# A hybrid decoder layer: the order in which stick-breaking's values are prepared, and the place at which a recurrence column's weights are rounded

## The chip, the cores and the metric

One core of a Trainium2 chip runs the whole layer as one program. The metric is the device time of one execution in microseconds (us). The engines are named as in the profile: PE (matrix products), PEld (the loading of its weights), DVE (vector), ACT (scalar: copies, casts, activations), POOL (GpSimd) and SP, whose queue issues most DMA transfers.

## The reference

A layer for 1024 tokens of width 1024, with 16 learned tokens (`META`) ahead of them, all in float32. Two feed-forward half steps enclose a mixer, whose single projection `W_in` feeds four recurrence heads (HGRN2) and eight attention heads (stick-breaking).

```python
h = h + 0.5 * swiglu(rms_norm(h, ffn1_norm), ffn1_w_in, ffn1_w_out)
u = rms_norm(h, mix_norm) @ w_in
hq, hf, hi, hg, sq, sk, sv = split(u)
o_hg = hgrn2(hq, hf, hi, hg, lb, hgrn_out_norm)   # S = diag(f) S + (1-f) v^T; o = S^T q
o_sb = stick_breaking(sq, sk, sv, sb_q_norm, sb_k_norm)
#   A[t,s] = sigmoid(z_ts) * prod_{s<j<t} (1 - sigmoid(z_tj)),  z = q.k / sqrt(d)
h = h + concat([o_hg, o_sb]) @ w_out
h = h + 0.5 * swiglu(rms_norm(h, ffn2_norm), ffn2_w_in, ffn2_w_out)
```

In the recurrence f goes through a sigmoid, q and g through x * sigmoid(x), and v enters as it is.

## The kernel before

**Precision.** A float32 product is made of three faster ones: each operand is split into a rounded high part and the rest (`wh`, `wl` for weights, `xh`, `xl` for activations), and PE adds xh·wh, xh·wl and xl·wh (lines 258 to 260). A weight tile is loaded by SP as `raw` (128x1024, line 236), rounded by ACT (`wh`, line 241, the cast spoken of below) and subtracted by DVE (`wl`, line 243). All of this is in `split_w`, which `col_tile` calls for one column tile of `W_in`, that is 128 output columns.

**Stages.** The program runs feed-forward 1 (to about 697 us), the first projections of the mixer, the stick-breaking projections for four pairs of heads p = 0 to 3 (to about 862 us; the last of them with the first recurrence columns), then a *braid* in which attention jobs and recurrence columns take turns on PE (to about 1126 us), a tail, `W_out` (from 1169 us) and feed-forward 2 (from 1280 us).

**Recurrence columns.** `hgrn_fill` goes through 16 columns: v, f, q and g of head 0, then of head 1, and so on (v0, f0, q0, g0, v1 ... g3). Tokens are taken in four `PIECES` for v and f (264, 264, 256, 256) and in two `HALVES` of 512 for q and g. Each piece is a product into one PSUM bank (`proj`), which ACT then empties into a staging tile `st`: a copy for v (line 1144), two sigmoids for f (1150, 1151), a sigmoid for q and g (1158), the last followed by DVE's product with the bank (1159). In the braid there is one such bank. When a column begins, `part` calls `col_tile` for the next column (at the first column for the next two), which loads, casts and subtracts its weights; `ahead_w` keeps them. There are 3 buffers for `wh` and `wl`, 2 for `raw`.

**Attention jobs.** PE makes scores z in one of two banks (1649 to 1652). ACT reads them twice (`keep` at 1655, `sig` at 1656), DVE scans `keep` (1659) and POOL multiplies both (1665). PE then *flips* the weights block by block (a transpose into one of two banks, 1504 and 1558), ACT rounds what it finds there (`wu` and `wm`, 1627), DVE subtracts (1628), and PE multiplies with the values (`oacc`, 1579 and 1581). `olow` and `ot` (1620, 1621) read the result out.

**The values.** `sb_v` is a generator for one pair p: it transposes the projected values `vTs` on DVE by groups of tokens (`vt`), casts them on ACT (`vhl`, 1446), subtracts on DVE (1447) and writes them to DRAM through SP (`vD`, 1454). Its groups are 512 tokens, 512 tokens, and last the 16 learned tokens (a tile of 128x32). Beside it `sb_qk` normalizes q and k and splits them (`ohi`, 1425). Each `yield` gives the turn to other work.

**What sets the order.** PE's instructions stay in the order in which the program lists them (a manual schedule). On the other engines a scheduler picks the order; `issue_after(x)` tells it that what follows comes on its queue behind x.

## Time and profile before

| | |
|---|---|
| median of 3 runs | 1964.71 us (1962.61 to 1965.23) |
| profiled execution | 1965.29 us, with a span of 1963.6 us in the trace |
| busy: PE, DVE, ACT, POOL | 1928.3, 1391.6, 851.7, 449.8 us |
| granted TensorE clock | 1.00 |
| casts at line 241 | 25, of 1052 ns each in the median |
| subtractions at line 243 | 25, of 1226 ns each in the median |

The span runs from the first to the last instruction of the trace; the execution's own time is 1.7 us longer. In a row of a timeline stand the start, the duration, the engine, the line, the operation, output <- inputs, the shapes and how often, and in brackets the idle time of the engine ahead of it with the instruction that ended it. In a row on a whole line stand the least, the median and the largest duration in ns.

### The profile page before, as it was taken

The page shows a single profiled execution, that of the slowest core. Times are in us where ns is not written, and L with a number is a line of the kernel's source. Part 1 is how long each engine was busy: PE and PEld are TensorE (multiplying, and loading weights), DVE is VectorE, ACT ScalarE, POOL GpSimd, SP SyncE. Part 2 cuts the span into 40 slices and gives each one's busy share as a digit, 9 for nine tenths or more (in the row PEclk, how much of TensorE's full clock was granted, in tenths as well). Part 3 has the DMA queues.
Part 4 walks back from the last instruction along what each step waited for, and adds up shares of the span by engine and source line. Part 5 has one row for each costly group of instructions (what it writes and reads, how often), then busy time and mean ns, then how long its engine had stood idle before and what let it go on. Part 6 is the DMA issues. An engine that isn't in the chain of part 4 may idle for free.

```text
span 1963.6 us, 30437 instructions
## 1 busy us (share of the span) xinstructions
PE 1928.3 (98%) x10704; PEld 1622.0 (83%) x10704; DVE 1391.6 (71%) x2186; ACT 851.7 (43%) x1711; POOL 449.8 (23%) x626
## 2 busy tenths in 40 slices
PE   7999999999999999999999999999999999999999
PEld 6888888888888888888888978887888888888887
DVE  6977777877678665567777766667567777767774
ACT  6523343334444544356666635433132332344443
POOL 3010100001000003133333332210544545430000
PEclk9999999999999999999999999999999999999999
DMA  6356787757965415865454167655544444469473
GB/s 211 93 160 174 245 278 237 235 208 280 372 226 185 136 47 144 194 175 148 126 143 126 57 249 216 171 204 181 195 117 140 126 137 119 134 236 330 146 232 113
DMA packets 381688, 355.56 MB, mean 181 GB/s; under 512 B 129040, under 2 KB 284560, under 8 KB 381536
## 3 DMA queue, kind: packets, MB, share of 16 engines
q1 hardware_dynamic: 359728, 288.98, 48.2%
q0 software_dynamic: 20768, 64.63, 9.5%
q8 instruction: 85, 1.39, 0.3%
q14 instruction: 67, 0.55, 0.1%
q10 hardware_dynamic: 1040, 0.00, 0.0%
HBM read 237.95 MB, written 115.57 MB: 180 GB/s over the span
## 4 chain that ended last, share of the span: by engine, by line
PE 91%; DVE 4%; DMA 2%; ACT 2%; issue 1%; POOL 0%; SPq 0%; ACTq 0%; DVEq 0%; POOLq 0%
PE o L741 21%; PE qb L459 18%; PE qc L459 12%; PE qa L459 12%; PE proj L258 5%; PE proj L260 5%; PE proj L259 5%; PE flip L1504 2%; PE wo L259 1%; PE wo L260 1%; PE wo L258 1%; PE mq L1010 1%; PE oacc L1579 1%; PE oacc L1581 1%; PE z L1649 1%
## 5 line engine op out<-in xcount | busy, mean ns | idle before, releaser
L459 PE MATMUL qb<-T,wh 128*128 128x512 f32 x1056 | 344.5, 390 | 1.3 <-ACT T L318 0.8
L459 PEld LDWEIGHTS qb<-T,wh 128*128 128x128 f32 x1056 | 198.1, 188 | 46.1 <-issue 2.5
L459 PE MATMUL qa<-B,wh 128*128 128x512 f32 x696 | 226.8, 391 | 0.0
L258 PE MATMUL proj<-xh,wh 128*128 128x512 f32 (+2 forms) x640 | 213.4, 333 | 2.4 <-ACT st L1151 1.3
L741 PE MATMUL o<-t,w 128*128 128x512 f32 x924 | 211.8, 390 | 0.5 <-DVE u L552 0.5
L260 PE MATMUL proj<-xl,wh 128*128 128x512 f32 (+2 forms) x640 | 209.8, 328 | 0.8 <-DVE xl L1973 0.8
L259 PE MATMUL proj<-xh,wl 128*128 128x512 f32 (+2 forms) x640 | 209.7, 328 | 0.0
L741 PE MATMUL o<-parts 128*128 128x512 f32 x924 | 209.6, 389 | 0.0
L459 PE MATMUL qb<-T,wl 128*128 128x512 f32 x528 | 205.4, 389 | 0.0
L741 PEld LDWEIGHTS o<-t,w 128*128 128x128 f32 x924 | 172.8, 188 | 37.3 <-issue 0.8
L741 PEld LDWEIGHTS o<-parts 128*128 128x128 f32 x924 | 173.4, 188 | 36.0
L371 DVE TENSOR_TENSOR wl<-s,wh 128x512 fp32r<-128x512 f32 x160 | 165.8, 1036 | 50.8 <-ACT wh L369 49.8
L369 ACT CAST wh<-s 128x512 fp32r<-128x512 f32 x160 | 99.7, 624 | 188.5 <-PE qb L459 142.3
L459 PEld LDWEIGHTS qa<-B,wh 128*128 128x128 f32 x696 | 130.6, 188 | 27.3 <-DVE B L845 0.3
L369 ACT CAST wh<-raw 128x512 fp32r<-128x512 f32 x120 | 74.6, 622 | 147.3 <-PE qc L459 99.0
L459 PE MATMUL qa<-B,wl 128*128 128x512 f32 x348 | 135.4, 389 | 0.0
L258 PEld LDWEIGHTS proj<-xh,wh 128*128 128x128 f32 x640 | 120.6, 188 | 14.5 <-ACT st L1151 2.0
L260 PEld LDWEIGHTS proj<-xl,wh 128*128 128x128 f32 x640 | 120.5, 188 | 12.1 <-DVE xl L1973 1.2
L259 PEld LDWEIGHTS proj<-xh,wl 128*128 128x128 f32 x640 | 120.5, 188 | 9.9
L459 PE MATMUL qc<-T,wh 128*128 128x512 f32 x352 | 117.0, 394 | 0.0
L459 PE MATMUL qc<-B,wh 128*128 128x512 f32 x352 | 115.1, 390 | 2.0 <-DVE u L552 1.2
L459 PEld LDWEIGHTS qb<-T,wl 128*128 128x128 f32 x528 | 99.1, 188 | 20.4
(398 smaller groups left out, 3853.9 us busy)
## 6 DMA issues: line engine op xcount, KB each, us to landing
raw<-in_ffn_w_in_dram SPq DMA_DIRECT2D x176, 256.0 KB, 3.9
raw<-in_ffn_w_out_dram SPq DMA_DIRECT2D x112, 256.0 KB, 4.4
w2in<-both SPq DMA_DIRECT2D x28, 512.0 KB, 3.4
raw<-in_w_in_dram SPq DMA_DIRECT2D x25, 512.0 KB, 5.1
ks<-kD SPq DMA_DIRECT2D x32, 260.0 KB, 4.7
wout<-both SPq DMA_DIRECT2D x16, 512.0 KB, 3.8
wh<-w2in SPq DMA_DIRECT2D x27, 256.0 KB, 3.5
wl<-w2in SPq DMA_DIRECT2D x27, 256.0 KB, 3.6
```

The lines of the kernel that those rows point to most:

```text
L258: nc.tensor.matmul(ps, wh[:, s], xs, start=k == 0, stop=False)
L259: nc.tensor.matmul(ps, wl[:, s], xs, start=False, stop=False)
L260: nc.tensor.matmul(ps, wh[:, s], xl[:, k, c0 : c0 + n], start=False, stop=k == nk - 1)
L369: nc.scalar.copy(hi, src)
L371: self.block_lo = nc.vector.tensor_sub(lo, src, hi.bitcast(F32))
L459: nc.tensor.matmul(ps, a[:, k, :], b[:, k, :], start=start and k == 0 and i == 0, stop=k == 3 and i == 2, skip_group_check=True,)
L741: nc.tensor.matmul(banks[bank][m], y[:, m * P : (m + 1) * P], z, start=start and at == 0 and e == 0, stop=q == nq - 1 and e == 2, skip_gro ...
L1010: nc.tensor.matmul(ps[at : at + 32, at_g, :], self.xm[:, 4 * h + k, :], got[i, h][:, k, :], start=h == 0 and kk == 0, stop=h == 1 and kk = ...
L1504: self.nc.tensor.transpose(ps[:m, j, :], src[:, s0 : s0 + m], self.ident)
L1579: nc.tensor.matmul(o[:, c], vj, w[0], start=j == 0, stop=False, skip_group_check=True)
L1581: nc.tensor.matmul(o[:64, c], vj[:, :64], w[1], start=False, stop=end, skip_group_check=True)
L1649: nc.tensor.matmul(z, q, ks[0][:, s0 : s0 + n], start=True, stop=False)
```

## The change

There are two edits. In `hgrn_fill` a column still has its weights loaded when its predecessor begins, always one column ahead now, but the cast and the subtraction are held back (`hold=True` makes `split_w` return a function). They are issued behind the instruction with which ACT empties the predecessor's second piece (v and f) or first half (q and g), which `self.emptied` names. In `sb_v` the learned tokens' group comes first instead of last, and gives up its two turns.

```diff
-    def split_w(self, view, parts=None):
+    def split_w(self, view, parts=None, hold=False):
...
-        hi = self.wp.tile([P, n], F32R, tag="wh", name="wh", bufs=self.w_bufs)
-        if self.split_on_vector:
-            nc.vector.tensor_copy(hi, raw)
-        else:
-            self.rounded = nc.scalar.copy(hi, raw)
-        lo = self.wp.tile([P, n], F32R, tag="wl", name="wl", bufs=self.w_bufs)
-        nc.vector.tensor_sub(lo, raw, hi.bitcast(F32))
-        return hi, lo
+
+        def split(after=None):
+            hi = self.wp.tile([P, n], F32R, tag="wh", name="wh", bufs=self.w_bufs)
+            with self.tc.issue_after(after) if after else ExitStack():
+                if self.split_on_vector:
+                    nc.vector.tensor_copy(hi, raw)
+                else:
+                    self.rounded = nc.scalar.copy(hi, raw)
+            lo = self.wp.tile([P, n], F32R, tag="wl", name="wl", bufs=self.w_bufs)
+            nc.vector.tensor_sub(lo, raw, hi.bitcast(F32))
+            return hi, lo
+
+        return split if hold else split()
...
             if kind == "v":
-                nc.scalar.copy(t, ps)
+                self.emptied = nc.scalar.copy(t, ps).ins
...
-                nc.scalar.activation(k, ps, AF.Sigmoid, scale=-1.0)
+                self.emptied = nc.scalar.activation(k, ps, AF.Sigmoid, scale=-1.0).ins
...
-                nc.scalar.activation(t, ps, AF.Sigmoid)
+                self.emptied = nc.scalar.activation(t, ps, AF.Sigmoid).ins
                 nc.vector.tensor_mul(t, t, ps)
...
-                for c in cols[i + 1 : i + (3 if i == 0 else 2)]:
+                for c in cols[i + 1 : i + 2]:
                     if c not in self.ahead_w:
-                        self.ahead_w[c] = self.col_tile(self.a["w_in"][0], c)
+                        self.ahead_w[c] = self.col_tile(self.a["w_in"][0], c, True)
...
             if half == 1:
                 with self.tc.issue_after(kept["round"]) if i == 0 else ExitStack():
                     use(*plan[i], kept["ps"], c0, n)
+                following = cols[i + 1] if i + 1 < len(plan) else None
+                if ci == (plan[i][0] in "vf") and callable(self.ahead_w.get(following)):
+                    self.ahead_w[following] = self.ahead_w[following](self.emptied)
...
-        for c0, nb, m in ((META, 16, 32), (META + 512, 16, 32), (0, 1, META)):
+        for c0, nb, m in ((0, 1, META), (META, 16, 32), (META + 512, 16, 32)):
...
-            yield 0, 800
+            if c0:
+                yield 0, 800
...
-            yield 0, 1500
+            if c0:
+                yield 0, 1500
```

PE's instructions stand in the same order before and after. On ACT, the place where f0's first pieces are emptied reads before (`ohi` and `vhl` belong to the last stick-breaking pair, `wh` is q0's weights, `st` from the bank are f0's pieces):

```order
L1446 CAST vhl<-vt 128x32
L1425 ACTIVATE ohi<-kT,kg 128x528
L241 CAST wh<-raw 128x1024
L1150 ACT_TABLE_LOAD
L1150 ACTIVATE st<-proj 128x264
L1151 ACTIVATE st<-proj 128x264
L1150 ACTIVATE st<-proj 128x264
L1151 ACTIVATE st<-proj 128x264
L1150 ACTIVATE st<-proj 128x256
```

and after (lines of the changed kernel, where 1150 and 1151 are 1155 and 1156):

```order
L1433 ACTIVATE ohi<-kT,kg 128x528
L1155 ACT_TABLE_LOAD
L1155 ACTIVATE st<-proj 128x264
L1156 ACTIVATE st<-proj 128x264
L1155 ACTIVATE st<-proj 128x264
L1156 ACTIVATE st<-proj 128x264
L244 CAST wh<-raw 128x1024
L1155 ACTIVATE st<-proj 128x256
```

The cast moved from ahead of the table load to behind f0's second piece, and the learned tokens' cast is gone from here.

On DVE, behind q0's first half (`st<-st,proj` is the column's product, the `keep` rows are the scans, `wu` and `wm` the subtractions for flips), before:

```order
L1628 TENSOR_TENSOR wu<-flip,wu 128x2x128
L1159 TENSOR_TENSOR st<-st,proj 128x512
L1659 SCALAR_TENSOR_TENSOR keep<-keep,idle 128x265
L1628 TENSOR_TENSOR wm_7907<-flip,wm_7906 16x256
L1659 SCALAR_TENSOR_TENSOR keep<-keep,idle 128x263
```

and after:

```order
L1638 TENSOR_TENSOR wu<-flip,wu 128x2x128
L1164 TENSOR_TENSOR st<-st,proj 128x512
L246 TENSOR_TENSOR wl<-raw,wh 128x1024
L1669 SCALAR_TENSOR_TENSOR keep<-keep,idle 128x265
L1638 TENSOR_TENSOR wm_7916<-flip,wm_7915 16x256
L1669 SCALAR_TENSOR_TENSOR keep<-keep,idle 128x263
```

The subtraction of g0's weights, which stood ahead of f0's last piece before, now stands between q0's product and the scans. The other columns of the braid follow the same pattern, on ACT behind the half or the piece and on DVE behind the column's own product.

More of the change, by code (lines that the diff above doesn't have):

```diff
@@ L236, in split_w, with col_tile @@
         self.last_load = nc.sync.dma_start(to, view)
-        hi = self.wp.tile([P, n], F32R, tag="wh", name="wh", bufs=self.w_bufs)
-        if self.split_on_vector:
-            nc.vector.tensor_copy(hi, raw)
-        else:
-            self.rounded = nc.scalar.copy(hi, raw)
-        lo = self.wp.tile([P, n], F32R, tag="wl", name="wl", bufs=self.w_bufs)
-        nc.vector.tensor_sub(lo, raw, hi.bitcast(F32))
-        return hi, lo
-    def col_tile(self, w, col):
+        def split(after=None):
[9 more added lines that the diff above has]
+        return split if hold else split()
+    def col_tile(self, w, col, hold=False):
         return self.split_w(
-            w[:, col : col + P].rearrange("(k p) f -> p k f", p=P), self.parted.get(col)
+            w[:, col : col + P].rearrange("(k p) f -> p k f", p=P), self.parted.get(col), hold
         )
```

## The prediction

> **What bounds the kernel now.** The first rows of the page say which engine is full.

> ```profile
> span 1963.6 us, 30437 instructions
> PE 1928.3 (98%) x10704; PEld 1622.0 (83%) x10704; DVE 1391.6 (71%) x2186; ACT 851.7 (43%) x1711; POOL 449.8 (23%) x626
> ```

> PE is busy for 1928.3 of 1963.6 us. The change touches the middle of the program only, so I next read the busy time of each engine by stage (columns: stretch, length, PE, PEld, DVE, ACT, POOL, granted clock, DMA share, GB/s).

> ```profile
> 732.00:862.00 130.00, 128.36 (x779) 114.46 (x779) 72.04 (x111) 58.18 (x111) 34.12 (x53) 1.00 0.66 166
> 862.00:1126.00 264.00, 256.96 (x1817) 228.16 (x1817) 192.81 (x310) 174.28 (x446) 94.77 (x137) 1.00 0.45 126
> 1126.00:1169.00 43.00, 41.04 (x254) 35.21 (x253) 23.84 (x71) 15.18 (x32) 18.54 (x46) 1.00 0.66 235
> ```

> These are the stick-breaking projections, the braid of attention jobs with recurrence columns, and its tail. PE is not busy for 1.64 + 7.04 + 1.96 = 10.6 us in them. ACT is free for a third of the braid (174.28 busy of 264), so ACT work as such costs nothing there; what counts is where it stands when PE next needs a result of ACT or DVE. PE's own waits from 862 to 1169 name these needs (us in total, times, longest):

> ```profile
> PE flip L1504 <- DVE wu L1628: 3.0, 7, 0.7
> PE flip L1504 <- DVE wm L1628: 1.5, 3, 0.6
> ...
> PE z L1649 <- ACT sig L1656: 1.2, 4, 0.5
> ```

> A flip (a transpose of the weights) waits until ACT and then DVE have emptied the flip before it; a z product waits until ACT has read the z two before it. Both chains run through bursts of small ACT and DVE instructions, and the change puts its work into such bursts.

> **The change part by part.** PE's order is unchanged, so its busy time stays, and only its waits can move. Moved are 14 of the 25 roundings of weights (those of the columns q0 to g3) with the subtraction behind each. The two lines over the whole trace, as least, median and most ns of one:

> ```profile
> L241 ACT CAST wh<-raw x25: 1037/1052/1088, 729.6 to 1107.7; 128x1024 fp32r<-128x1024 f32 x25
> L243 DVE TENSOR_TENSOR wl<-raw,wh x25: 1178/1226/2139, 731.0 to 1108.7; 128x1024 fp32r<-128x1024 f32 x25
> ```

> So each move carries 1.05 us of ACT and 1.23 of DVE from one place to another. A place costs PE nothing where the engine would idle; it costs up to 1.05 where ACT is in a chain PE waits for, and up to about 1.5 where the subtraction then stands ahead of DVE's part of the chain too.

> *What leaves.* First, f0's opening piece. The rows in order of time:

> ```profile
> 853.54 1.04 ACT L241 CAST wh<-raw 128x1024 fp32r<-128x1024 f32 x1
> 854.60 1.28 ACT L1150 ACT_TABLE_LOAD   x1
> ...
> 856.18 0.38 ACT L1151 ACTIVATE st<-proj 128x264 f32<-128x264 f32 x1
> ...
> 856.62 0.39 PE L258 MATMUL proj<-xh,wh 128*128 128x256 f32 x1 [1.32 <-ACT st L1151]
> 858.08 0.39 ACT L1151 ACTIVATE st<-proj 128x264 f32<-128x264 f32 x1 [1.23 <-DMA hg_v<-st]
> ```

> PE waits 1.32 for the sigmoid at 856.18, which stands behind the table load, which stands behind q0's cast. That cast now comes behind f0's second piece (the sigmoid at 858.08), so the load can begin at 853.54 rather than 854.60. PE's last matmul before the wait is not moved, so the wait falls to about 0.3: −1.0. The load begins 0.02 us after the cast ends and the sigmoid follows 0.01 behind the load (854.60 + 1.28 = 855.88 against a start of 855.89 on the page's timeline of ACT), so nothing else stands between them.

> [...]

> Next, two old places where the subtraction held DVE ahead of a flip, g1's and g3's:

> ```profile
> 931.17 1.81 POOL L1665 TENSOR_TENSOR sig<-sig,keep 128x912 f32<-128x912 f32 x1 [2.94 <-DVE keep L1659]
> 931.92 2.14 DVE L243 TENSOR_TENSOR wl<-raw,wh 128x1024 fp32r<-128x1024 f32 x1 [0.92 <-ACT wh L241]
> 936.95 0.30 PE L1504 MATMUL flip<-ident,sig 128*128 128x128 f32 x1 [0.67 <-DVE wu L1628]
> 1108.74 1.23 DVE L243 TENSOR_TENSOR wl<-raw,wh 128x1024 fp32r<-128x1024 f32 x1 [0.50 <-ACT wh L241]
> 1111.26 0.41 PE L1504 MATMUL flip<-ident,sig 128*128 128x128 f32 x2 [0.59 <-DVE wm L1628]
> ```

> Without 2.14 and 1.23 us ahead of them, DVE reaches both flips' inputs earlier than PE needs them: −0.67 and −0.59, −1.3 together. What is late next is PE itself. Two more subtractions (q1's, g2's) stand a few us ahead of smaller such waits; I take −0.5 for both, out of the 3.0 that all seven hold. The other old places lie in idle time of ACT or DVE and give nothing.

> Last, the values' generator. The learned tokens' cast (128x32) now comes between the copies of the values' projection, and a copy of kT that PE waits for gets ahead of a long split:

> ```profile
> 780.70 0.19 PEld L258 LDWEIGHTS proj<-xh,wh 128*128 128x128 f32 x1 [0.34 <-ACT kT L1387]
> ```

> That is −0.4 with the slow first matmul behind it. Its four stores move ahead on SP's queue, past the last store of v0's column, which lets that store leave earlier; the work there has cover, and I take 0. The gains are −1.0 − 1.3 − 0.5 − 0.4 = −3.2.

> *What arrives.* Behind the first half of a q or g column and the second piece of a v or f column, ACT now does the cast at once. Behind it are queued, on ACT, the reads of z and the emptyings of flips, and on DVE, behind the subtraction, the products that release the next flip. q0's first half is the clearest place:

> ```profile
> 874.25 0.39 ACT L1655 ACTIVATE keep<-z 128x264 f32<-128x264 f32 x1
> ...
> 874.97 0.42 PE L1649 MATMUL z<-ks,qs 128*128 128x328 f32 x1 [0.48 <-ACT sig L1656]
> ```

> The row of ACT shows no wait before it: the engine goes from the column's half to z without a gap. PE already waits 0.48 for the sigmoid that follows. The cast's 1.05 go straight into the wait: +1.05. Two more bursts are of this kind, behind g0's and q1's first halves, where the z after next starts as the sigmoid ends:

> ```profile
> 897.13 0.55 ACT L1656 ACTIVATE sig<-z 128x456 f32<-128x456 f32 x1
> 897.73 0.43 PE L1649 MATMUL z<-ks,qs 128*128 128x348 f32 x1
> ...
> 964.78 0.54 ACT L1656 ACTIVATE sig<-z 128x456 f32<-128x456 f32 x1
> 965.38 0.43 PE L1649 MATMUL z<-ks,qs 128*128 128x348 f32 x1
> ```

> The sigmoids end at 897.68 and 965.32, 0.05 before the products: +1.0 each.

> Behind g1's, g2's and q3's halves it is DVE's product that PE needs next:

> ```profile
> 984.94 0.68 DVE L1628 TENSOR_TENSOR wu<-flip,wu 128x512 fp32r<-128x512 f32 x1
> 985.68 0.39 PE L1558 MATMUL flip<-ident,sig 128*16 128x128 f32 x2
> ...
> 1073.10 0.42 DVE L1628 TENSOR_TENSOR wu<-flip,wu 128x256 fp32r<-128x256 f32 x1
> 1073.66 0.30 PE L1504 MATMUL flip<-ident,sig 128*128 128x128 f32 x1 [0.61 <-DVE wu L1628]
> ...
> 1140.32 0.41 DVE L1628 TENSOR_TENSOR wm<-flip,wm 16x256 fp32r<-16x256 f32 x1
> 1140.79 0.33 PE L1581 MATMUL oacc<-wm,v 128*64 128x256 f32 x1 [0.26 <-DVE wm L1628]
> ```

> The first of these products ends 0.06 before its flip. With the cast (1.05) and then the subtraction (1.23) ahead of it, less the 0.7 to 0.8 that DVE spends anyway on the column's own product, it comes some 1.5 later: +1.4 for each, +4.2.

> The rest are smaller. I estimate them from the same two prices, 1.05 and 1.4, less the slack that the timelines of PE and DVE leave there. f2's second piece is followed by two flips of which the later needs DVE's product: +0.9. At f1, f3 and q2 the slack takes most: +0.3 each. Behind the pieces of v1, v2 and v3 ACT idles next: 0. That is +1.8; the ends for these seven are 0 and 7 x 1.05 = 7.4. q0's weights are late enough to watch: the sigmoid of 858.08 ends at 858.47, so cast and subtraction end near 860.8, and q0 follows on PE behind f0's last two pieces, some 5.8 us behind the row of 856.62, or 861.4 when 1.0 is saved; I take 0, at 1.0 per us if the load lands late.

> The losses are 1.05 + 2.0 + 4.2 + 1.8 = 9.05, so the net is −3.2 + 9.05 = +5.9 on the profiled execution. Its time was 1965.29 us (span 1963.6 and 1.7 around it), 0.6 over the median of 1964.71. A change in waits carries over to the median: 1964.7 + 5.9 = 1970.6. Some of a new wait is made up, since waits that already follow shrink while DVE catches up; I take 0.6 off for that and forecast 1970.0.

> **The rivals.**

> *The casts hide, and DVE's waits go (faster).* The new place is a fixed one, right after PE has freed the bank and gone on with the next piece. If PE's two z's and the projection matmuls behind them cover 1.05 us, no new wait comes. It decides at the 0.05 us between sigmoid and z at 897.73: the rows speak against it, the free third of ACT for it. Then the gains stand alone, and with the subtractions gone from ahead of the flips up to all of 3.0 + 1.5 go instead of 1.8: −3.2 to −5.9, middle −4.5, or 1960.2.

> *Half of it hides.* Only the places where PE waits already (874.97, 1073.66, 1140.79) lose: 1.05 + 1.4 + 1.4 = 3.85, net +0.6, or 1965.3. For it: these are rows with a wait before, the others are starts that are just in time.

> *Every place loses, and the subtraction stretches.* 14 casts at 1.05 make 14.7. The 2.14 us at 931.92 ran beside POOL's product (931.17 to 932.98), 0.91 over the median; at a few of the new places such a product runs too, and each would add that. −3.2 + 14.7 + 0.9 = +12.4, or 1977. Against it: ACT idles behind the v pieces.

> [...]

> That the change doesn't do what it says is excluded by the order: all 14 casts stand behind their copies.

> **How the numbers follow.** A run can tell about 0.2% from no change, 3.9 us: faster is under 1960.8, slower over 1968.6. Chances: forecast 0.50 (1967 to 1973, of which 0.07 lies under 1968.6), hidden 0.24 (0.15 of it under 1960.8), half 0.18, every place 0.08. Faster 0.15; same 0.07 + 0.09 + 0.18 = 0.34; slower 0.43 + 0.08 = 0.51. The range takes the forecast, the half and the upper part of the hidden case: 1960.8 to 1974.0, which leaves out about 0.15 + 0.07.

> **What would show it.** In the profile after, the wait at f0's second piece is near 0.3 instead of 1.32; z waits of about 1 us stand behind q0's, g0's and q1's first halves; flips wait 1 to 2 us for DVE behind g1's and g2's; PE's total from ACT sig grows from 1.2 to some 4, and the three stages together lose about 6 us while the stages before 732 and after 1169 keep theirs. If z at q0's half waits no longer than 0.5, the hidden case is right and the forecast wrong. If the stages outside change by over 1 us, something that I don't see is at work.

## The result and the profile after

The changed kernel takes 1974.01 us in the median of 6 runs (1969.88 to 1975.10); the kernel before takes 1964.24 (1961.94 to 1966.23). The ratio is 1.0046, with a 95% interval from 1.0033 to 1.0059. The forecast was 1970.0: slower, as foreseen, but by 9.8 us instead of 5.3, above the forecast's own band (1967 to 1973) and at the upper edge of the range. The profiled execution took 1975.1 us, with a span of 1973.4.

The page after, in the two rows that were shown of before:

```profile
span 1973.4 us, 30439 instructions
PE 1933.1 (98%) x10704; PEld 1625.5 (82%) x10704; DVE 1391.0 (70%) x2186; ACT 851.0 (43%) x1711; POOL 448.8 (23%) x626
```

The span grew by 9.8 us, and 4.8 us of it are *busy* time of PE, although PE has the same instructions in the same order. Waits alone don't make PE busy for longer. I come back to this below.

PE's waits from 862 us on (total, times, longest), after:

```profile
PE flip L1514 <- DVE wu L1638: 5.1, 7, 2.1
PE z L1659 <- ACT sig L1666: 3.4, 6, 1.4
PE flip L1568 <- DVE wu L1638: 1.6, 1, 1.6
...
PE oacc L1591 <- DVE wu L1638: 0.9, 1, 0.9
PE flip L1514 <- DVE wm L1638: 0.9, 2, 0.5
```

Flips waited 3.0 + 1.5 for DVE before and wait 5.1 + 1.6 + 0.9 now; z went from 1.2 to 3.4. The single places on PE's timeline, in the order of the prediction's terms (f0, then q0's start, then the new places behind q0, g0, q1, g1, g2 and q3):

```profile
854.12 0.39 PE L263 MATMUL proj<-xh,wh 128*128 128x256 f32 x1 [0.98 <-ACT st L1156]
860.70 0.50 PE L263 MATMUL proj<-xh,wh 128*128 128x512 f32 x1 [0.41 <-ACT st L1156]
...
874.01 0.42 PE L1659 MATMUL z<-ks,qs 128*128 128x328 f32 x1 [1.42 <-ACT sig L1666]
...
897.56 0.43 PE L1659 MATMUL z<-ks,qs 128*128 128x348 f32 x1 [0.68 <-ACT sig L1666]
...
966.06 0.43 PE L1659 MATMUL z<-ks,qs 128*128 128x348 f32 x1 [0.68 <-ACT sig L1666]
987.84 0.39 PE L1568 MATMUL flip<-ident,sig 128*16 128x128 f32 x2 [1.57 <-DVE wu L1638]
...
1079.88 0.30 PE L1514 MATMUL flip<-ident,sig 128*128 128x128 f32 x1 [2.08 <-DVE wu L1638]
...
1148.59 0.33 PE L1591 MATMUL oacc<-wu,v 128*64 128x256 f32 x1 [0.94 <-DVE wu L1638]
```

The six large new waits stand where the prediction put them. f0's wait is 0.98 where it expected about 0.3, and a few smaller waits, such as 0.69 at 951.79 (0.23 before) and 0.21 at 1018.28, are not in it. The rest of the loss is in the clock. These rows are 3.4 us long each, in pairs: ahead of and behind three moments of the changed kernel (columns: stretch, length, busy time of PE, PEld, DVE, ACT, POOL, granted clock, DMA share, GB/s):

```profile
985.60:989.00 3.40, 1.53 (x11) 0.93 (x9) 3.15 (x5) 3.35 (x9) 0.01 (x1) 1.00 0.57 176
989.00:992.40 3.40, 3.01 (x11) 2.65 (x12) 2.82 (x6) 1.55 (x5) 2.19 (x2) 0.50 0.47 133
1077.80:1081.20 3.40, 1.26 (x8) 0.86 (x8) 3.10 (x6) 2.84 (x9) 0.28 (x1) 1.00 0.35 119
1081.20:1084.60 3.40, 3.00 (x9) 2.57 (x10) 1.77 (x4) 1.02 (x3) 3.32 (x4) 0.50 0.60 189
1146.10:1149.50 3.40, 1.91 (x14) 1.26 (x12) 3.01 (x5) 2.25 (x5) 0.00 (x0) 0.99 0.20 77
1149.50:1152.90 3.40, 3.40 (x9) 2.72 (x10) 2.42 (x15) 0.77 (x2) 2.04 (x2) 0.50 0.34 116
```

Behind each of the three places where cast *and* subtraction stand ahead of DVE's product, the clock is halved, to 0.50, for 3.4 us. From 17 us to the last matmul it is nowhere else under 0.99. By these two figures a stretch loses at most 1.7 us. PE's products are longer in it: one of 128x512 at line 264 takes 0.63 us at 991.06, inside, and 0.40 at 993.08, behind it. Set side by side, instruction by instruction, PE's two timelines drift apart by 1.35, 1.37 and 1.46 us in these stretches, 4.2 together. In the kernel before, the same place behind g2's half had a wait of 0.61 and kept its clock:

```profile
1071.60:1075.00 3.40, 2.70 (x19) 1.90 (x17) 2.45 (x5) 3.01 (x9) 0.28 (x1) 1.00 0.20 77
1075.00:1078.40 3.40, 3.02 (x15) 2.59 (x16) 1.66 (x4) 0.99 (x3) 3.32 (x4) 1.00 0.23 77
```

The stretches don't come in every run. The six runs of the changed kernel have a mean clock of 0.997 (1975.10 and 1974.36 us), 0.998 (1973.67 and 1974.65) and 1.000 (1970.90 and 1969.88). A stretch of 3.4 us at half clock takes 0.0009 off the mean (1.7 of some 1970 us), so I take these to be three, two and none; the run of 1975.10 is the profiled one, with its three. The two runs without one lie 6.1 us above the median of before (1970.39 against 1964.24).

### The profile page after: what moved, and what is told of

It is laid out like the page before. It is cut to its first block, busy times and chain, and to the rows that moved or that the text cites. A ratio compares the mean times of both kernels' runs of the same rounds, so it can differ in the third digit from the quotient of the medians.

```text
span 1973.4 us, 30439 instructions
## 1 busy us (share of the span) xinstructions
PE 1933.1 (98%) x10704; PEld 1625.5 (82%) x10704; DVE 1391.0 (70%) x2186; ACT 851.0 (43%) x1711; POOL 448.8 (23%) x626
## 4 chain that ended last, share of the span: by engine, by line
PE 90%; DVE 4%; ACT 2%; DMA 1%; issue 1%; POOL 1%; SPq 0%; DVEq 0%; ACTq 0%; POOLq 0%
PE o L746 21%; PE qb L464 18%; PE qc L464 12%; PE qa L464 12%; PE proj L263 5%; PE proj L265 5%; PE proj L264 5%; PE flip L1514 1%; PE wo L264 1%; PE wo L265 1%; PE wo L263 1%; PE mq L1015 1%; PE oacc L1589 1%; PE oacc L1591 1%; PE z L1659 1%
```

## The experiments

Theory A: the loss comes from the held roundings, as waits at the places named, and as the halved clock behind the longest of them. The rivals were that the moved stores of the values cost the time (B), that the halved clock is a matter of chance and not of waits (C), that POOL and DVE hinder each other (D), and that f0's gain is lost to late weights (E). "Shift" below is the start of an instruction of PE in the experiment less its start in the kernel before; only the differences of shifts along the program are used.

**Each edit alone.** `e1` is the kernel before with the new `sb_v`; `e2` is the changed kernel with the old one.

```diff
 # e1
-        for c0, nb, m in ((META, 16, 32), (META + 512, 16, 32), (0, 1, META)):
+        for c0, nb, m in ((0, 1, META), (META, 16, 32), (META + 512, 16, 32)):
 # e2: the changed kernel, with this line and the two yields turned back
```

> Only the values' edit (learned tokens' group first); the roundings stay free as before. Theory A (the loss comes from the held roundings): within 1.5 us of before; the wait at kT (0.34 at 780.70 before) is gone, the wait at f0's second piece stays about 1.3 less 0.2 for the small cast, no stretch of halved clock. Rival B (the moved stores and the earlier small cast are what costs): 4 us or more slower.

> Only the held roundings; the values' group of the learned tokens stays last. Theory A: 5 to 10 us slower than before, as the changed kernel, with the same waits (z 1.4 behind q0's half; flips 1.6 and 2.1 behind g1's and g2's) and up to three stretches of halved clock. Rival B: at most 3 us slower.

`e1`: 1964.74 us, ratio 1.0003 (0.9994 to 1.0013), so the values' edit makes no difference that can be told. `e2`: 1974.47 us, ratio 1.0054 (1.0037 to 1.0071), the whole loss. Rival B falls. In `e1` the kT wait went as forecast (shift −0.38 by 781 us), and a wait at q0's start took it back and more (+1.24). One expectation missed: the clock was halved for 7 us in the profiled execution of `e1` (1198 to 1205), behind a wait of 1.41 us for a load of `W_out`'s weights; that execution is the slowest of its ten runs, seven of which have a mean clock of 1.000.

`e2` shows f0's term by itself:

```profile
852.81 0.38 PE L263 MATMUL proj<-xh,wh 128*128 128x256 f32 x1 [0.40 <-ACT st L1156]
859.80 0.50 PE L263 MATMUL proj<-xh,wh 128*128 128x512 f32 x1 [0.83 <-ACT st L1156]
...
858.14 1.05 ACT L244 CAST wh<-raw 128x1024 fp32r<-128x1024 f32 x1 [2.69 <-DMA raw<-in_w_in_dram]
```

With the cast gone from ahead of the table load, f0's wait is 0.40 instead of 1.32. The cast, now behind f0's second piece, then waits 2.69 for its load, which is issued one column ahead instead of two, and holds the sigmoids of f0's next pieces behind it on ACT. PE waits 0.83 for the bank.

In the changed kernel the same wait fell to 0.98 only. What ACT does ahead of the table load is the split of kT (`ohi`), and that waits until a store has read the buffer it writes to. The rows of the kernel before, of `e2` and of the changed kernel:

```profile
852.90 0.74 ACT L1425 ACTIVATE ohi<-kT,kg 128x528 fp32r<-128x528 f32 x1 [1.98 <-DMA qD<-ohi]
```

```profile
850.04 0.74 ACT L1433 ACTIVATE ohi<-kT,kg 128x528 fp32r<-128x528 f32 x1 [2.00 <-DMA qD<-ohi]
```

```profile
851.35 0.74 ACT L1433 ACTIVATE ohi<-kT,kg 128x528 fp32r<-128x528 f32 x1 [2.86 <-DMA qD<-ohi]
```

The split starts 2.40, 2.37 and 1.79 us ahead of the moment at which PE runs out of work. With q0's cast gone from behind it, `e2` gains all of 0.9; in the changed kernel the store lands later and takes 0.6 of that back. `e2` and the changed kernel differ in the values' edit alone, so it is this edit that costs the 0.6.

**The three places.** `e3` frees the weights of v2, v3 and g3 in the changed kernel; `e4` holds only these three in the kernel before.

```diff
 # e3
-                        self.ahead_w[c] = self.col_tile(self.a["w_in"][0], c, True)
+                        self.ahead_w[c] = self.col_tile(
+                            self.a["w_in"][0], c, plan[i + 1] not in (("v", 2), ("v", 3), ("g", 3)))
 # e4: the same with "in", the load of two columns ahead at the start, and the old sb_v
```

> The changed kernel, but the weights of v2, v3 and g3 are rounded where the scheduler likes; the other 11 stay held. Theory A (each halved-clock stretch follows from one of these three places, where cast and subtraction stand ahead of DVE's product): the three waits of about 1.5 go (some 4.2 us), the clock is 1.00 in every run and the 1.7 us per stretch go too; in all 4 to 9 us faster than the changed kernel, +1 to +2 against before. Rival C (the halved clock is a state of the chip that comes whatever the waits are): the clock is under 1.00 in some runs still, and only the 4.2 us come back.

> The kernel before, with only the weights of v2, v3 and g3 held behind g1's, g2's and q3's first halves; the other 11 and the values as before. Theory A: +4 in waits at the three places, and 1.7 more for each stretch of halved clock (up to three): 4 to 9 us slower than before, the clock 0.997 to 1.00. Rival C: +4 at most, clock 1.00 as before. If the crowding of all 14 places together is what counts, less than +2.

`e3`: 1969.36 us, ratio 1.0025 (1.0015 to 1.0034), 4.7 us faster than the changed kernel. The clock was 1.00 in all ten runs, and they lie within 2.8 us. But not all of the three waits came back: the freed casts found other places, with waits of 0.84 at 970.82 and 1.25 at 1059.28, so that by the shifts the stage's waits fell by only about 2 us. What `e3` saved is mostly the clock (4.2 in the trace of the changed kernel). That it would come to +1 or +2 against before was wrong; it is +5.0.

`e4`: 1971.66 us, ratio 1.0035 (1.0025 to 1.0046), so three held columns of 14 cost 7.3 us by themselves. With the 5.0 of `e3` that is more than the loss of the changed kernel, so the parts don't simply add up: the three roundings that `e3` frees cost time at other places. All three places of `e4` have their stretch:

```profile
987.30:990.70 3.40, 2.78 (x10) 2.52 (x11) 3.34 (x6) 2.53 (x7) 1.24 (x1) 0.52 0.44 130
1079.20:1083.00 3.80, 3.34 (x12) 2.64 (x11) 3.11 (x6) 1.55 (x5) 3.37 (x2) 0.55 0.51 155
1147.10:1151.10 4.00, 3.73 (x11) 2.94 (x11) 3.09 (x20) 1.09 (x3) 1.94 (x2) 0.60 0.29 98
```

Its runs fall into two groups: three with a mean clock of 0.999, as one stretch makes it (1967.63 to 1969.21, 1968.4 in the mean), and five with 0.997, as three make it (1971.31 to 1973.73, 1972.5 in the mean). Two more stretches go with 4.1 us.

**Cast or subtraction.** `e5` gives the held subtractions of the changed kernel to POOL; the casts stay. `e6` does the same to the kernel before.

```diff
-            nc.vector.tensor_sub(lo, raw, hi.bitcast(F32))
+            (nc.gpsimd if hold else nc.vector).tensor_sub(lo, raw, hi.bitcast(F32))
 # e6: the same for the kernel before, with a flag of its own for these columns
```

> The changed kernel with the 14 held subtractions (wl) on POOL instead of DVE; the casts stay where the change put them. Theory A (cast and subtraction both stand ahead of DVE's product behind g1's, g2's and q3's halves: about 1.05 of cast, 0.5 of subtraction): the flip waits there fall by about 0.5 each, to 1.0 and 1.5, the z waits (1.42, 0.68, 0.68) stay, and with less idle time in a row the halved clock comes less often: 3 to 6 us faster than the changed kernel. Rival D (POOL's subtraction and DVE's work exclude each other): no gain, or slower.

> The kernel before, its order of casts untouched, with the subtractions of the columns' weights on POOL. Theory A (the old places of g1's, q1's, g2's and g3's subtractions cost PE 0.9, 0.3, 0.3 and 0.7 us): these waits go, 1 to 2 us faster than before, at the limit of what can be told. Rival D: the same or slower, since the subtraction takes POOL longer or holds DVE.

`e5`: 1966.08 us, ratio 1.0013 (1.0004 to 1.0022), 8 us faster than the changed kernel and more than expected. POOL's subtraction takes twice as long as DVE's (2390 ns in the median against 1225 in the changed kernel), and nobody waits for it for long:

```profile
L246 POOL TENSOR_TENSOR wl<-raw,wh x14: 2361/2390/2410, 856.2 to 1139.9; 128x1024 fp32r<-128x1024 f32 x14
```

```profile
PE z L1659 <- ACT sig L1666: 3.4, 6, 1.4
PE flip L1514 <- DVE wu L1638: 3.4, 6, 1.2
...
PE flip L1568 <- DVE wu L1638: 0.9, 1, 0.9
```

The z waits (the cast's alone) stay at 3.4, the longest flip wait falls from 2.1 to 1.2, that behind g1 from 1.6 to 0.9, and the clock is 1.00 throughout the profiled execution and in seven of the ten runs (0.999 in three). So the subtraction was 0.6 to 0.9 us of the long waits. From 862 to 1169 us PE's shift grows by 2.6 us here and by 12.0 in the changed kernel: of the 9.4 between them 4.2 are the clock and some 5 are waits, many of them short. Rival D falls. `e6`: 1963.26 us, ratio 0.9997 (0.9988 to 1.0006). Its flips gained some 2.2 us in shift (at 913, 937, 952, 1021 and 1111), but at the braid's start z waited 1.7 in sum and the clock was halved there for 7 us, without any rounding being held; nine of its eleven runs have a mean clock of 0.999 or 0.998. The gain can't be told from no change.

**How long a wait must be.** `e7` holds only g0's, v1's and g1's weights (the z places), `e8` only v3's (one place), `e11` as `e8` with the subtraction done twice.

```diff
 # e7: plan[i + 1] in (("g", 0), ("v", 1), ("g", 1));   e8: plan[i + 1] in (("v", 3),)
 # e11, to e8:
             nc.vector.tensor_sub(lo, raw, hi.bitcast(F32))
+            if hold:
+                nc.vector.tensor_sub(lo, raw, hi.bitcast(F32))
```

> The kernel before with only g0's, v1's and g1's weights held, behind q0's, g0's and q1's first halves, the places where a z product waits for the cast. Theory A: waits of 1.4, 0.7 and 0.7 at z, +2.6 against before less 0.9 for g1's old place; none of them is followed by a stretch of halved clock, so 1 to 3 us slower. Rival C' (any wait over about 0.7 us can set off the halved clock): a stretch behind one of the three places.

> The kernel before with only v3's weights held, behind g2's first half (one place). Theory A: the flip there waits 2.1 instead of 0.6 and one stretch of halved clock of about 3.4 us follows within 2 us of it, which costs 1.7: 1.5 to 3.5 us slower in all. Rival C: the wait without the stretch, +1.5.

> The kernel before with only v3's weights held (as in the run with one place) and the subtraction done twice, so that the flip behind g2's half waits 1.2 us longer, some 3.3 us. Theory A (a long wait sets off the halved clock): a stretch of halved clock of some 3.4 us behind it in the trace, 1.7 us lost, and 4 to 6 us slower than before in all. Rival C (the stretch comes by chance and not by the wait): clock 1.00 at this place and 3 us slower.

`e7`: 1967.30 us, ratio 1.0019 (1.0010 to 1.0028). z waits 1.42, 0.67 and 0.68, and the profiled execution has no stretch; eight of the ten runs have a mean clock of 1.000. It is 3.4 us slower than before, more than the 1 to 3 expected, and flips wait 0.81 twice at 902.63 and 970.97, which wasn't foreseen. `e8`: 1966.46 us, ratio 1.0015 (1.0006 to 1.0024), 2.6 us slower than before, as expected. The wait is the 2.08 of the changed kernel, but in the profiled execution the clock stays at 1.00; there the expectation of a stretch missed. Other runs had one: seven of the ten have a mean clock of 0.999 or 0.998, against 4 of the 33 runs of the kernel before that were taken with them (where in the program it stood, the mean doesn't say). `e11`: 1968.50 us, ratio 1.0022 (1.0013 to 1.0031), with 0.999 or 0.998 in all ten runs. The second subtraction was queued ahead of the next flip's product, so that two waits follow each other, 2.08 and 1.46. Around the place, 3.4 us of `e8`:

```profile
1073.00:1076.40 3.40, 1.27 (x9) 0.86 (x8) 3.09 (x6) 3.35 (x10) 0.00 (x0) 1.00 0.36 124
```

and of `e11`, with what follows:

```profile
1072.00:1075.40 3.40, 1.32 (x10) 0.87 (x8) 3.13 (x5) 3.35 (x9) 0.00 (x0) 0.98 0.20 77
1075.40:1082.00 6.60, 5.14 (x16) 4.03 (x15) 5.31 (x7) 1.50 (x4) 4.59 (x5) 0.50 0.43 128
```

PE is busy for 1.3 of 3.4 us in both. One keeps its clock, the other has it halved for twice 3.4 us. What differs in the two traces is where the wait falls on a beat. In each of the 14 traces every change of the granted clock comes a whole number of steps of 3.4133 us behind its first rise, to within 0.004 us; in the changed kernel, for instance, the rise is at 16.23 (24 transposes from 11.03 on take 5.34 us, 8 from 19.31 on take 1.19), and 989.03, 1081.19 and 1149.46 are 285, 312 and 332 steps behind it. That rise lies anywhere from 13.80 to 17.12 us, so the beat falls differently on the program in each execution. Cut on its beat, `e8` (rise at 15.84) has the wait split over two steps:

```profile
1070.56:1073.97 3.41, 2.45 (x16) 1.83 (x14) 2.22 (x3) 2.13 (x4) 0.62 (x2) 1.00 0.00 0
1073.97:1077.38 3.41, 1.84 (x13) 1.47 (x14) 3.35 (x6) 3.39 (x10) 0.85 (x1) 1.00 0.66 214
```

and `e11` (rise at 17.12) has it whole in one, with the halved clock in the next:

```profile
1071.83:1075.24 3.41, 1.33 (x11) 0.94 (x10) 3.17 (x4) 3.36 (x8) 0.00 (x0) 1.00 0.20 77
1075.25:1078.66 3.41, 1.95 (x8) 1.49 (x8) 3.35 (x7) 1.65 (x5) 2.05 (x2) 0.50 0.63 188
```

So in these two the halved clock goes with a wait, as A has it, and with where the beat falls on it (1.33 us busy in one step, against 2.45 and 1.84 in two), which differs from execution to execution: that is the part of C that holds.

**What became of f0's gain, and a version out of the parts.** `e9` is the changed kernel with f's two outputs of a piece in one staging tile. `e10` is the kernel before with POOL's subtractions, only q0's rounding held (its load two columns ahead as before) and that tile. `e12` is the kernel before with POOL's subtractions for v1 to g3 only.

```diff
 # e9, e10
-            return pool.tile([P, 512], F32, tag="st", name="st", bufs=4)[:, :n]
+            return pool.tile([P, 528], F32, tag="st", name="st", bufs=4)[:, :n]
...
-            t = staged(n)
+            t = staged(2 * n if kind == "f" else n)
...
-                k = staged(n)
+                t, k = t[:, :n], t[:, n:]
 # e12: e6, with the flag True only for i > 2
```

> The changed kernel with f's two outputs of a piece in one staging tile (528 wide, four of them), so that f0's third piece finds a free one. Theory A (f0's earlier sigmoids were given back because ACT waited 4.06 us for a store of hg_k to free a staging tile, and PE 0.41 for the bank at q0): that wait of ACT shrinks to under 1.5 and PE's wait at q0's first matmul goes; f0 to q0 is 0.6 us shorter than in the changed kernel, with no more than 1 us in the whole time. Rival E (the weights of q0 are late, from their later load): the wait at q0 stays, now for the subtraction.

> Put together from what the runs showed to gain: the kernel before with the columns' subtractions on POOL, only q0's rounding held behind f0's second piece, its load two columns ahead as before, and the wider staging tile. Theory A: the waits ahead of flips go (2.0 in sum) and f0's falls from 1.3 to 0.4: 2 to 3 us faster than before. Rival D or E: no gain, since a load or a store takes the place of the wait.

> The kernel before, its casts where they were, with the subtractions of 12 of the columns (v1 to g3) on POOL; q0's and g0's stay on DVE, since with those on POOL too the braid's first z products waited 1.7 us in sum. Theory A: the waits ahead of the flips that the subtractions of q1, g1, g2 and g3 caused go (2.0 us in sum), and nothing takes their place at the braid's start: 1.5 to 2.5 us faster than before, clock 1.00 throughout the stage. Rival: the gain is taken up by another wait there, within 0.5 us of before.

`e9`: 1973.37 us in three runs, ratio 1.0047 (1.0032 to 1.0062), as the changed kernel. PE's wait at q0 is gone: the shift from f0's wait to q0 stays, where the changed kernel lost 0.58. So in the changed kernel the staging tiles took back what was left of f0's gain. Rival E falls for the changed kernel; the late load shows in `e2`. ACT still waits 2.68 there, not under 1.5, but PE no longer feels it. `e10`: 1963.17 us, ratio 0.9996 (0.9987 to 1.0005). f0's wait is 0.39 as expected, and then a free cast takes its place:

```profile
855.90 0.39 PE L263 MATMUL proj<-xh,wh 128*128 128x256 f32 x1 [0.39 <-ACT st L1156]
...
867.27 0.47 PE L1657 MATMUL z<-ks,qs 128*128 128x456 f32 x1 [1.48 <-ACT sig L1664]
...
865.59 1.04 ACT L244 CAST wh<-raw 128x1024 fp32r<-128x1024 f32 x1 [2.59 <-DMA raw<-in_w_in_dram]
```

g0's cast waits 2.59 for its load in front of the z reads, and PE 1.48 behind it; from 870.07 the clock is halved for 3.4 us, and all eleven runs have a mean clock of 0.999 or 0.998. The 2 to 3 us that were expected are not there. `e12`: 1961.81 us, ratio 0.9990 (0.9981 to 0.9999), 1.9 us faster than before. The flip waits fell about as forecast, by 1.7 us in sum:

```profile
PE flip L1504 <- DVE wu L1628: 1.9, 4, 0.7
...
PE z L1649 <- ACT sig L1656: 1.1, 4, 0.5
PE flip L1504 <- DVE wm L1628: 0.9, 2, 0.5
```

They were 3.0, 1.2 and 1.5 in the kernel before. This is the one version that beats both, at the limit of what can be told. In the stage the theory held: no wait took their place, and the clock there is 1.00. The profiled execution had one stretch of halved clock all the same, in feed-forward 1 (226 to 229), which the edit doesn't touch, behind a wait of 1.99 us there.

## Why the prediction was right, and where it was off

The side and the mechanism of the waits were right, and most terms came out within 0.5 us. In shifts of PE, forecast against measured:

| term | forecast | measured |
|---|---|---|
| f0's sigmoid ahead of the cast, to q0's start | −1.0 | −0.36 + 0.58 = +0.2 |
| copy of kT at 780.70 | −0.4 | −0.4 |
| old places of g1, g3 | −1.3 | −0.87 − 0.69 = −1.6 |
| old places of q1, g2 | −0.5 | −0.28 − 0.36 = −0.6 |
| z behind q0, g0, q1 | +3.05 | +0.96 + 0.79 + 0.87 = +2.6 |
| DVE's product behind g1, g2, q3 | +4.2 | +1.48 + 1.55 + 1.55 = +4.6 |
| behind f1, f2, f3, q2 | +1.8 | +0.56 + 0.94 + 0.25 + 0 = +1.8 |
| elsewhere in the braid (951.98; 1014.31, a piece of v2) | 0 | +0.57 + 0.46 = +1.0 |
| halved clock | not foreseen | +4.2 |

Without the clock the measured column sums to +7.6, of which about 0.7 is regained in the tail (behind 1165 us); the forecast had +5.9. So the three stages, from 732 to 1169 us, lost 11.2 us: 7.0 in waits and 4.2 in the clock, where the prediction named about 6. It also said that the stages outside would keep their times. Behind 1169 us that holds (+0.3), but ahead of 732 the profiled execution of the changed kernel is 1.7 us faster, in short waits of feed-forward 1. The kernels are the same there, and among the profiled executions of the experiments without a halved clock in that stage the shift at 732 us lies anywhere from −2.85 to +0.22, so I take this as scatter. Single profiles can't be compared more finely than that over the whole program.

**The step that was missed** is the one from waits to time. The prediction took PE's busy time as given ("PE's order is unchanged, so its busy time stays, and only its waits can move"). In the profiled execution the matmuls behind three long waits were also slower, at a clock of 0.50: PE was busy for 4.8 us more with the same instructions. The two runs without a halved clock lie 6.1 us over before, close to the waits' sum of +5.9; in the other four the clock adds up to some 5. That the median is still within the range is partly luck, since it hangs on how many stretches six runs happened to have. The stretches are gone in all ten runs of `e3` and most of `e5`, and they return in `e4` and `e11`, so in the changed kernel they come from the pile of cast and subtraction behind one half, not from the number of held columns. The pile is one way to such a wait and not the only one: `e6` and `e10` have the halved clock behind z waits at the braid's start.

**f0's term** had the right size where it arises (`e2`: 1.32 to 0.40) and the wrong end. "What is late next" was asked of PE only. Three kinds of transfers were: q0's load, one column ahead instead of two (`e2`), the store ahead of kT's split (the changed kernel, 0.6), and the stores that free f0's staging tiles (the changed kernel; `e9` takes that away). The prediction had priced the late load at q0 as a risk and taken 0. That DMA took the gain is shown by `e2` and `e10`, where f0's wait did fall by the 0.9 (1.32 to 0.40 and 0.39).

**The rivals.** That the casts hide is refuted by the z waits of 1.42 and 0.68. That half of them hides too. That every place loses is refuted at v1's and v3's pieces, behind which PE has no wait; behind v2's, also put at 0, there is a small one (0.21). The stretched subtraction hardly occurred (the longest is 1828 ns in the changed kernel). No rival had the clock in it.

## What to carry to other kernels

Work that is held behind a fixed instruction lands in whatever burst follows that instruction; look for the tightest chain behind it on each engine, and keep a cast and its subtraction from standing in the same chain (giving the subtraction to POOL, busy for 23% of the span, saved 8 us here). Price a long wait of PE at more than its length: where the trace shows the clock halved behind such waits, it can cost as much again (here three waits, longer by 1.5 us each, cost 4.6 and then 4.2 more). When a step is sped up, ask what is late next on the queues of loads and stores as well as on PE.

## What was not expected of the hardware

The clock was halved behind waits much shorter than the stretch itself: in the changed kernel 2.08, and 1.57 with 0.69 behind it, against 3.4 us. In the traces of these kernels it went to 0.50 for 3.4 us, or for twice that, within some 3 us behind a wait, or a group of waits, that left PE busy for 1.3 to 2.2 of 3.4 us. This wasn't bound to the change: `e12` has it in feed-forward 1, `e1` behind a late load of `W_out`. It is not certain either. Behind g2's half, with 1.3 of 3.4 us busy, it came in the profiled executions of the changed kernel, `e2`, `e4`, `e9` and `e11`, and not in that of `e8`; behind q0's half, with 2.0 busy in `e7`, it came in no profiled execution.
